# Output passes summed on TensorE by an identity product, gate and residual in the last pass, and five input buffers in place of a staging pool

## The chip, the core and the metric

The kernel runs on one core of one Trainium2 chip. A core has five engines that run side by side: TensorE (PE: matrix products; PEld: the loading of their weights), VectorE (DVE), ScalarE (ACT), GpSimd (POOL) and SyncE (SP), which here issues every DMA, all through one queue. The metric is the device time of one execution in microseconds.

## The reference, cut to what matters

One layer of a hybrid diffusion backbone: a shared input projection, eight head groups ("slots") that each hold a gated DeltaNet head of 128 channels and two RWKV-7 heads of 64, in both directions over time, and a shared output projection. The 256 context tokens pass first and leave the recurrent state from which the 512 latent tokens go on.

```python
h  = rmsnorm(x, norm_g) * (1 + scale) + shift        # 512 x 2048
hc = rmsnorm(ctx, norm_g) * (1 + scale_c) + shift_c  # 256 x 2048
u, uc = h @ w_in, hc @ w_in
ya_c, ya = gdn_mixer(uc[:, :GDN_COLS], u[:, :GDN_COLS], ...)
yb_c, yb = rwkv_mixer(uc[:, GDN_COLS:], u[:, GDN_COLS:], ...)
x = x + gate * (concat([ya, yb]) @ w_out)            # 512 x 2048
return rmsnorm(x, final_norm_g)
```

Only the latent tokens are returned, so the context tokens have no output projection.

## The kernel before, in words

**Layout.** Channels lie on the partitions, tokens in the free dimension. A big product is split for precision: weights and data are each a high and a low part (`wh`, `wl`; `hhi`, `hlo`; `yh`, `yl`), and three products `hi*hi + hi*lo + lo*hi` are added up in PSUM, for every block of 128 input channels, as 128 x 512 pieces.

**Who sets the order.** The code does not write instructions directly. Every call is recorded as an operation with its data dependences, and a planner (`Rec.schedule`) then sorts the operations of each engine by a simulated start time from its own tables of costs; `emit` writes them out in that order. So all instructions have the one line L705, and the order on an engine is fixed by the planner. Each engine runs its list strictly in order. Three tables matter here: `LAT` holds what the planner adds when one engine waits for another, `OWN` what it adds when an operation waits for an earlier one on its own engine (before: V, A and G only, so a DMA that waits for another DMA is planned as if it could go at once), and the `warm` operation: where the planner sees TensorE's recent activity fall below a level it puts in small filler products of zeros (`wm<-zero`).

**Phases.** The front makes the modulation, the norms and the small projections (to some 150 us). The context phase (to some 1000 us) computes the projections `Gk, Gv, Rk, Rv` of every slot for both streams and runs the eight context mixers. The latent phase takes the other projections and the eight latent mixers, slots 0 to 7.

**A mixer** (`Mix`) has these steps: `prep_g`, `prep_r`, `prep_d 0/1`, `blocks 0/1` make small matrices in the tile `Z`; `send` writes their diagonal blocks to DRAM (`DA`); `solve` reads them back (`solNL<-DA`), inverts them on VectorE with 60 dependent elementwise operations (`solT`, `solNL`) and writes the result to DRAM (`DD<-solNL`); `levels` loads it (`lt<-DD`, `Z<-DD`) and finishes the inverses; `chain` walks the eight chunks of time, a serial ping-pong of TensorE, ScalarE, VectorE and GpSimd; `outp` normalizes and stores the result `y`. Two "lanes" of buffers let two neighbouring slots overlap.

**The inputs of a latent mixer.** A projection job (`proj`) collects its sum in PSUM, finishes it in a staging tile (`ul`, a pool of two buffers) and writes it to DRAM (`ud`). Some jobs are done in two parts, and part 1 loads part 0 back into the staging tile. `u_load` loads the six inputs of a slot, in the order Rk, Gk, Rr, Gv, Gq, Rv, into the pool `u` of three buffers (traced as `Rk`).

**The output projection** is cut into four passes over the input channels, each a sweep over the 16 blocks of output channels; pass p takes two slots' channels. Passes 0, 1, 2 are queued after slots 3, 5, 6 as work to fill holes, pass 3 after slot 7's chain in program order, and `out_last` does the last slot. Passes 0 to 2 take for each block an evacuation on ScalarE that also scales by the gate (`xt<-accl`), a load of the running sum (`xr`, in pass 0 of the input x), an addition on GpSimd (`xt<-xt,xr`) and a store (`rtd<-xt`). The same passes split their weights on GpSimd (`wl<-wr,wh`). Pass 3 loads the sum into `rt` and adds its part on VectorE.

Of the kernel before, what the change touches and what calls it, by code (L numbers as in the profile page):

```python
# [7 lines left out]
F32 = mybir.dt.float32  # L8
# [7 lines left out]
P = 128  # L16
# [132 lines left out]
OWN = {"V": 120, "A": 148, "G": 107}  # L149
# [1091 lines left out]
class Kernel:  # L1241
# [51 lines left out]
    def setup(self):  # L1293
# [3 lines left out]
        self.hl = self.pool("hl", side="right")  # L1297
        self.hc = self.pool("hc", side="right")
# [60 lines left out]
    def front(self):  # L1359
# [59 lines left out]
        for kt in range(KT):  # L1419
# [12 lines left out]
            ar = fp.tile([P, 256], F32, tag="ar", bufs=2, name=self.nm("ar"))  # L1432
# [40 lines left out]
        self.ul = self.pool("ul")  # L1473
# [104 lines left out]
    def bcast_rows(self, dst, col, nj, ones, pool, psum):  # L1578
        for g in range(0, nj, 4):
            m = min(4, nj - g)  # L1580
            ps = psum(g // 4)
            for j in range(m):
                dg = pool.tile([P, P], F32, tag="dg", bufs=2, name=self.nm("dg"))
                self.V.tensor_scalar_mul(dg, self.cs("ident"), col[:, g + j:g + j + 1])
                self.mm(ps[:, 128 * j:128 * j + 128], ones, dg)
            self.act(dst[:, 128 * g:128 * (g + m)], ps[:, 0:128 * m], AF.Copy)
# [14 lines left out]
    def proj(self, kind, i, ctx, lat, part=None):  # L1601
# [19 lines left out]
        if lat:  # L1621
            t = self.ul.tile([P, SEQ], F32, tag="ul", bufs=2, name=self.nm(kind))
# [25 lines left out]
    def u_load(self, kind, i):  # L1648
        tag = "uz" if kind[1] == "z" else "u"
        t = self.u[(kind, i, 1)] = self.mp.tile([P, SEQ], F32, tag=tag, bufs=(3, 1)[tag == "uz"], name=self.nm(kind))  # L1650
        self.S.dma_start(t, self.u_d[JOBS.index(kind), i])
# [87 lines left out]
    def main(self):  # L1739
# [27 lines left out]
        for i in range(NSLOT):  # L1767
# [5 lines left out]
            if i == n0:  # L1773
                self.hl.release()
# [46 lines left out]
    def out_pass(self, p):  # L1821
# [5 lines left out]
        for i in range(KT):  # L1827
# [4 lines left out]
            else:  # L1832
                o = 2 * (i % 2)
                if o == 0:
                    hi, lo = self.split(self.I["wout"][24 + 8 * p + i // 2].rearrange("p (k m) -> p k m", m=P), eng)
            for k in range(n):
                for m, (w, hx) in enumerate(((hi, yh), (hi, yl), (lo, yh))):
                    self.mm(ps, w[:, o + k], hx[:, k], k == 0 and m == 0, k == n - 1 and m == 2)
            g = self.dvo["gt"][:, i:i + 1]
            if p == 3:  # L1840
                r = self.rt[:, i]
                self.S.dma_start(r, self.rt_d[:, i])
                self.stt(r, ps, g, r, ALU.mult, ALU.add)
                continue
            x, r = (self.xp.tile([P, SEQ], F32, tag=t, bufs=2, name=self.nm(t)) for t in ("xr", "xt"))
            self.S.dma_start(x, self.rt_d[:, i] if p else self.I["xt"][:, i, 0:SEQ])
            self.act(r, ps, AF.Copy, scale=g)
            self.tt(r, r, x, ALU.add, self.G)
# [60 lines left out]
    def close(self):  # L1909
# [4 lines left out]
        self.ul.release()  # L1914
# [27 lines left out]
```

## Time and profile before

| | us |
|---|---|
| time, median of 3 runs (lowest to highest) | 2160.66 (2158.78 to 2163.45) |
| time of the profiled execution | 2166.2 |
| its span, first to last instruction | 2164.4 |
| PE busy | 1966.3 (91%) |
| DVE busy | 1475.2 (68%) |
| ACT busy | 815.9 (38%) |
| POOL busy | 640.2 (30%) |
| DMA packets' share of the 16 engines | 41.8% |

The span is the stretch between the first and the last instruction of the profiled execution; its time is the span and 1.8 us around it. "Busy" is the share of the span in which an engine had an instruction of the program under way. PE's 91% holds the filler products too, so it must be read by stage.

### The profile page before, as it was taken

What the parts mean: (1) busy time and instruction counts of PE and PEld (TensorE: products, weight loads), DVE (VectorE), ACT (ScalarE), POOL (GpSimd) and SP (SyncE); (2) the same over time, 40 slices, a digit from 0 to 9 for tenths busy, and PEclk for the clock granted to TensorE, in tenths of its full rate; (3) what the DMA queues carried; (4) which work ended last, traced back from release to release, by engine and by line L of the source; (5) the groups of instructions that cost most, each with busy time, mean ns of one, the idle gap of its engine ahead of it and who ended that gap; (6) DMA issues with size and microseconds to landing.
All of it is one profiled execution on the core that took longest, in us unless ns stands there. A gap on an engine that the chain in (4) does not pass through costs nothing.

```text
span 2164.4 us, 44432 instructions
## 1 busy us (share of the span) xinstructions
PE 1966.3 (91%) x16999; PEld 1542.0 (71%) x17000; DVE 1475.2 (68%) x3397; ACT 815.9 (38%) x2127; POOL 640.2 (30%) x799
## 2 busy tenths in 40 slices
PE   7999999999999999999999999978887897889877
PEld 5678887777877778776777777756665666667666
DVE  6436578675867769574765865786868577767747
ACT  4443333333242433324434434436424452435235
POOL 0003404213140421101212202235823564246226
PEclk8999999999999999999999999999979899899998
DMA  8964433333333333344541542544631544044702
GB/s 305 358 221 109 114 92 95 94 89 88 95 98 90 103 101 88 84 114 124 143 133 47 157 128 67 177 140 143 202 87 44 150 154 136 24 123 123 229 12 97
DMA packets 230517, 269.33 MB, mean 124 GB/s; under 512 B 117280, under 2 KB 130080, under 8 KB 226208
## 3 DMA queue, kind: packets, MB, share of 16 engines
q1 hardware_dynamic: 230304, 266.49, 41.8%
q8 instruction: 133, 2.18, 0.4%
q14 instruction: 80, 0.66, 0.1%
HBM read 210.50 MB, written 55.89 MB: 123 GB/s over the span
## 4 chain that ended last, share of the span: by engine, by line
PE 51%; DVE 22%; DMA 12%; issue 5%; SPq 5%; ACT 3%; POOL 3%; DVEq 0%; ACTq 0%; POOLq 0%
PE accl L705 23%; PE wm L705 8%; PE pss L705 7%; PE br L705 7%; PE accc L705 6%; DVE solNL L705 6%; SPq L705 5%; DVE solT L705 4%; DMA DD<-solNL 3%; DVE Gk L705 3%; DVE wl L705 2%; DMA DA<-Z 1%; DVE t L705 1%; DMA solNL<-DA 1%; DMA yl<-yd 1%
## 5 line engine op out<-in xcount | busy, mean ns | idle before, releaser
L705 ACT ACTIVATE wh<-wr 128x512 fp32r<-128x512 f32 x312 | 196.1, 629 | 375.5 <-PE accc L705 144.3
L705 PE MATMUL accl<-hhi,wl 128*128 128x512 f32 x768 | 317.1, 413 | 10.9 <-DVE wl L705 10.9
L705 PE MATMUL accl<-hhi,wh 128*128 128x512 f32 x768 | 314.1, 409 | 1.8 <-issue 1.8
L705 PE MATMUL accl<-hlo,wh 128*128 128x512 f32 x768 | 312.7, 407 | 0.0
L705 DVE TENSOR_TENSOR wl<-wr,wh 128x512 fp32r<-128x512 f32 x264 | 187.6, 713 | 106.9 <-ACT wh L705 102.5
L705 PE MATMUL accl<-yh,wh 128*128 128x512 f32 x480 | 199.3, 418 | 22.0 <-ACT yh L705 13.8
L705 PE MATMUL accl<-yl,wh 128*128 128x512 f32 x480 | 198.7, 414 | 0.1
L705 PE MATMUL accl<-yh,wl 128*128 128x512 f32 x480 | 197.1, 412 | 1.5 <-DVE wl L705 0.9
L705 PEld LDWEIGHTS accl<-hhi,wl 128*128 128x128 f32 x768 | 146.9, 191 | 50.9 <-DVE wl L705 13.3
L705 DVE TENSOR_TENSOR solNL<-solNL,solT 48x30 f32<-48x30 f32 (+29 forms) x480 | 175.2, 365 | 10.3
L705 DVE TENSOR_TENSOR solT<-solNL 48x30 f32<-48x30 f32 (+29 forms) x480 | 170.6, 355 | 9.0
L705 POOL TENSOR_TENSOR SRd<-Sbd,Dd 64x128 f32<-64x128 f32 x160 | 71.1, 444 | 354.2 <-DVE Sbd L705 348.1
L705 PE MATMUL wm<-zero 128*128 128x128 bf16 x1846 | 146.2, 232 | 30.3 <-DVE SG L705 15.0
L705 PEld LDWEIGHTS accl<-hhi,wh 128*128 128x128 f32 x768 | 146.9, 191 | 20.6 <-issue 4.3
L705 PEld LDWEIGHTS accl<-hlo,wh 128*128 128x128 f32 x768 | 147.0, 191 | 20.2 <-issue 3.2
L705 PEld LDWEIGHTS <-zero 128*128 128x128 bf16 x1864 | 124.4, 105 | 51.7 <-issue 46.6
L705 PE MATMUL accc<-clo,wh 128*128 128x256 f32 x512 | 149.9, 293 | 0.0
L705 PE MATMUL accc<-chi,wh 128*128 128x256 f32 x512 | 147.6, 288 | 0.0
L705 PE MATMUL accc<-chi,wl 128*128 128x256 f32 x512 | 145.9, 285 | 0.0
L705 PEld LDWEIGHTS accl<-yh,wh 128*128 128x128 f32 x480 | 90.9, 191 | 43.2 <-ACT yh L705 15.0
L705 PEld LDWEIGHTS accc<-clo,wh 128*128 128x128 f32 x512 | 97.3, 190 | 24.1 <-issue 0.9
L705 PEld LDWEIGHTS accc<-chi,wh 128*128 128x128 f32 x512 | 97.3, 190 | 21.5 <-issue 0.7
(312 smaller groups left out, 4207.8 us busy)
## 6 DMA issues: line engine op xcount, KB each, us to landing
wr<-win SPq DMA_DIRECT2D x256, 256.0 KB, 3.2
wa<-wada SPq DMA_DIRECT2D x32, 1024.0 KB, 6.0
ud<-Gk SPq DMA_DIRECT2D x72, 256.0 KB, 2.6
gw<-wada SPq DMA_DIRECT2D x64, 256.0 KB, 3.5
wr<-wout SPq DMA_DIRECT2D x64, 256.0 KB, 2.9
Rk<-ud SPq DMA_DIRECT2D x48, 256.0 KB, 3.2
rtd<-xt SPq DMA_DIRECT2D x48, 256.0 KB, 2.2
xr<-rtd SPq DMA_DIRECT2D x32, 256.0 KB, 3.0
```

The lines of the kernel that those rows point to most:

```text
L705: r = getattr(self.engs[o.eng], o.fn)(*args, **kw)
```

## The change

Five edits go together.

1. Passes 1, 2 and 3 first load the running sum into `xr` and add it to the PSUM sum by a product with the identity matrix (`accl<-Rr,cst`; `xr` carries the name `Rr` in the new build), 48 products of 128 x 512 in plain fp32. The evacuation no longer scales, the addition on GpSimd is gone, and pass 0 loads nothing.
2. Gate and residual come once, in pass 3, which now loads the input x into `rt` and does `rt = ps * gate + rt`.
3. The pool `u` has five buffers instead of three. The room comes from the staging pool, which is closed when slot 3 begins; part 1 of a projection job stages in `xr`.
4. The planner's table `OWN` gets 1500 ns for S: a DMA that needs an earlier DMA's data is planned later.
5. `ar` and the `dg` tiles of the front have one buffer instead of two.

```diff
-OWN = {"V": 120, "A": 148, "G": 107}
+OWN = {"V": 120, "A": 148, "G": 107, "S": 1500}
...
+        self.ul = self.pool("ul", side="right")
...
-            ar = fp.tile([P, 256], F32, tag="ar", bufs=2, name=self.nm("ar"))
+            ar = fp.tile([P, 256], F32, tag="ar", bufs=1, name=self.nm("ar"))
...
-                dg = pool.tile([P, P], F32, tag="dg", bufs=2, name=self.nm("dg"))
+                dg = pool.tile([P, P], F32, tag="dg", bufs=1 + (pool.name == "fin"), name=self.nm("dg"))
...
-            t = self.ul.tile([P, SEQ], F32, tag="ul", bufs=2, name=self.nm(kind))
+            pool, tag = (self.xp, "xr") if part == 1 else (self.ul, "ul")
+            t = pool.tile([P, SEQ], F32, tag=tag, bufs=2, name=self.nm(kind))
...
-        t = self.u[(kind, i, 1)] = self.mp.tile([P, SEQ], F32, tag=tag, bufs=(3, 1)[tag == "uz"], name=self.nm(kind))
+        t = self.u[(kind, i, 1)] = self.mp.tile([P, SEQ], F32, tag=tag, bufs=(5, 1)[tag == "uz"], name=self.nm(kind))
...
             if i == n0:
+                self.ul.release()
...
+            if p:
+                x = self.xp.tile([P, SEQ], F32, tag="xr", bufs=2, name=self.nm("xr"))
+                self.S.dma_start(x, self.rt_d[:, i])
+                self.mm(ps, self.cs("ident"), x, True, False)
             for k in range(n):
                 for m, (w, hx) in enumerate(((hi, yh), (hi, yl), (lo, yh))):
-                    self.mm(ps, w[:, o + k], hx[:, k], k == 0 and m == 0, k == n - 1 and m == 2)
+                    self.mm(ps, w[:, o + k], hx[:, k], not p and k == 0 and m == 0, k == n - 1 and m == 2)
             g = self.dvo["gt"][:, i:i + 1]
             if p == 3:
                 r = self.rt[:, i]
-                self.S.dma_start(r, self.rt_d[:, i])
+                self.S.dma_start(r, self.I["xt"][:, i, 0:SEQ])
                 self.stt(r, ps, g, r, ALU.mult, ALU.add)
                 continue
-            x, r = (self.xp.tile([P, SEQ], F32, tag=t, bufs=2, name=self.nm(t)) for t in ("xr", "xt"))
-            self.S.dma_start(x, self.rt_d[:, i] if p else self.I["xt"][:, i, 0:SEQ])
-            self.act(r, ps, AF.Copy, scale=g)
-            self.tt(r, r, x, ALU.add, self.G)
+            r = self.xp.tile([P, SEQ], F32, tag="xt", bufs=2, name=self.nm("xt"))
+            self.act(r, ps, AF.Copy)
             self.S.dma_start(self.rt_d[:, i], r)
```

The planner sorts the whole program anew, so much moves. Counted over the whole lists: the filler products fall from 1846 to 1326, GpSimd loses its 48 additions, TensorE gains the 48 identity products, and the other instructions are the same ones in another order. Three places show how.

**VectorE where the chain of slot 2 ends.** `SV`, `SG`, `VO` are slot 2's chain (its last copy is `SV<-pss`), `ot` its output step, `solT`/`solNL` the solve of slot 3; a solve's rows grow from 96x30 to 96x240 in its middle and shrink to 96x30 again at its end. Before:

```order
L705 TENSOR_TENSOR SG_1_9315<-SGs_0_9317,pss_0_125 128x128
L705 TENSOR_TENSOR Ktok_0_9331<-br_1_130,rk_0_9302 128x512
L705 TENSOR_TENSOR solT_1425<-solNL_1424 96x240
L705 SCALAR_TENSOR_TENSOR VO_0_9332<-wm_0_124,SGN_73,VO_0_9332 128x128 x2
L705 TENSOR_TENSOR solNL_1424<-solNL_1424,solT_1425 96x16x15
L705 COPY SV_0_9345<-pss_0_125 64x128
L705 TENSOR_TENSOR solT_1425<-solNL_1424 96x240
L705 TENSOR_TENSOR solNL_1424<-solNL_1424,solT_1425 96x15x16
L705 TENSOR_TENSOR ot_0_9325<-accc_1_135,osb_0_9313 128x512
```

The same place after:

```order
L705 TENSOR_TENSOR solT_1428<-solNL_1427 96x30
L705 TENSOR_TENSOR Sbd_1429<-SRd_0_9340,pss_0_130 64x2x64 x2
L705 TENSOR_TENSOR SG_0_9338<-SGs_0_9341,wm_0_129 128x128
L705 TENSOR_TENSOR SG_1_9339<-SGs_0_9341,pss_0_130 128x128
L705 TENSOR_TENSOR Ktok_0_9355<-br_1_135,rk_0_9326 128x512
L705 TENSOR_TENSOR solNL_1427<-solNL_1427,solT_1428 96x30
L705 COPY solNL_1427<-solNL_1427 96x1024
L705 SCALAR_TENSOR_TENSOR VO_0_9356<-wm_0_129,SGN_73,VO_0_9356 128x128 x2
L705 COPY SV_0_9369<-pss_0_130 64x128
L705 TENSOR_TENSOR ot_1_9350<-accc_1_140,osb_0_9337 128x512
```

Before, half of slot 3's solve (31 of its 63 instructions) stands behind the end of slot 2's chain; after, the whole solve stands ahead of it. At the end of slot 6's chain the same holds for slot 7's solve: 41 of 63 behind it before, none after. The counts for slots 4, 5 and 6 behind the chain of the slot ahead of them are 17, 43, 17 before and 37, 21, 27 after.

**TensorE in slot 7's chain.** One of the eight chunks, its middle part: `Xs`, `R`, `SV`, `vt` feed the chain's products, `zero` is the filler, `accl` the bank of the output passes. Before:

```order
L705 MATMUL accc_0_134<-vn_0_9322,Z_0_12641 64x128 x2
L705 LDWEIGHTS zero_0_65
L705 MATMUL wm_0_124<-zero_0_65 128x128
L705 MATMUL pss_0_125<-Xs_0_9318,Z_0_12641 64x64 x4
L705 MATMUL wm_0_124<-R_1590_0_9319,Z_0_12641 64x128
```

After:

```order
L705 MATMUL accc_1_140<-vn_0_9346,Z_0_12502 64x128 x2
L705 MATMUL accl_0_144<-Rr_0_12489,cst_60 128x512
L705 MATMUL pss_0_130<-Xs_0_9342,Z_0_12502 64x64 x4
L705 MATMUL wm_0_129<-R_1590_0_9343,Z_0_12502 64x128
```

An identity product of pass 3 stands where a filler stood, ahead of the chain's next products. Before, pass 3 lay wholly ahead of slot 7's chain; after, 53 products of the passes (10 of them the rest of pass 2) and 8 identity products lie between the starts of the first and the last chunk of that chain, and 53 and 8 behind the start of the last (counted on TensorE's list).

**SyncE between slot 4's solve and its levels.** `DD` is the solve's result on its way out, `lt` and `Z` its way back in. Before:

```order
L705 DMA DD_0_119<-solNL_1424 96x2x1024
L705 DMA lt_0_9312<-DD_0_119 32x12x32
```

After:

```order
L705 DMA DD_0_124<-solNL_1427 96x2x1024
L705 DMA DA_1_123<-Z_0_12502 32x12x32
L705 DMA rtd_117<-xt_1_12492 128x512
L705 DMA wr_2_1435<-wout 128x512
L705 DMA Rr_0_12489<-rtd_117 128x512
L705 DMA rtd_117<-xt_0_12491 128x512
L705 DMA wr_0_1433<-wout 128x512
L705 DMA wup_0_9318<-wup 96x512
L705 DMA lr_0_9325<-lorad_114 96x512
L705 DMA lt_0_9336<-DD_0_124 32x12x32
```

Before, nothing stood between the two in any of the eight latent slots; after, there are 2, 3, 6, 1, 8, 5, 5 and 3 DMA issues in slots 0 to 7, some of which wait for ScalarE, TensorE or GpSimd.

## Rows read from the trace of the kernel before

**Rows 1.** Busy time by stretch, all engines: two stretches ahead of the output passes.

```profile
core 0: us, PE busy (x) PEld busy (x) DVE busy (x) ACT busy (x) POOL busy (x), PEclk, DMA share, GB/s
50.00:100.00 50.00, 50.00 (x449) 32.40 (x448) 24.54 (x56) 20.62 (x39) 0.00 (x0) 1.00 0.96 361
...
1300.00:1350.00 50.00, 50.00 (x473) 36.34 (x473) 26.95 (x79) 22.71 (x65) 11.25 (x24) 1.00 0.21 58
```

**Rows 2.** The same view cut at latent chains; columns as above; the sum spans 1469:2055.

```profile
1390.00:1469.00 79.00, 60.95 (x629) 47.12 (x630) 67.38 (x144) 31.95 (x86) 20.40 (x24) 0.94 0.56 164
...
1530.00:1603.00 73.00, 60.23 (x637) 47.47 (x636) 51.79 (x80) 21.81 (x50) 43.74 (x37) 0.88 0.58 169
1603.00:1658.00 55.00, 43.55 (x519) 32.97 (x518) 42.38 (x128) 26.52 (x92) 17.00 (x32) 0.91 0.14 40
...
1835.00:1893.00 58.00, 45.98 (x517) 34.85 (x518) 42.15 (x128) 26.74 (x94) 17.30 (x33) 0.85 0.13 38
...
1989.00:2055.00 66.00, 58.34 (x495) 45.11 (x494) 48.55 (x84) 16.83 (x35) 21.32 (x17) 0.93 0.68 218
2055.00:2103.00 48.00, 37.66 (x475) 28.75 (x474) 17.91 (x68) 14.91 (x43) 8.33 (x20) 0.91 0.01 2
2103.00:2164.40 61.40, 45.09 (x453) 42.95 (x452) 44.66 (x74) 33.58 (x87) 37.92 (x37) 0.87 0.30 95
...
sum 586.00, PE 499.28 PEld 381.41 DVE 421.05 ACT 234.78 POOL 276.67; mean PE 49.93 PEld 38.14 DVE 42.10 ACT 23.48 POOL 27.67
```

**Rows 3.** Instructions of the solve alone (tile solT), by stretch: DVE busy (count).

```profile
1530.00:1603.00 73.00, 19.68 (x31) 0.88 0.58 169
1603.00:1658.00 55.00, 15.73 (x44) 0.91 0.14 40
...
1760.00:1835.00 75.00, 22.99 (x42) 0.93 0.52 153
...
1989.00:2055.00 66.00, 20.55 (x40) 0.93 0.68 218
```

**Rows 4.** DVE and POOL instructions in order of time: start, us, what.

```profile
1539.10 1.49 DVE L705 TENSOR_TENSOR solT<-solNL 96x234 f32<-96x234 f32 x1
...
1538.87 1.46 POOL L705 TENSOR_TENSOR xt<-xt,xr 128x512 f32<-128x512 f32 x1
```

**Rows 5.** Groups by form: busy us, mean ns of one, idle before and its cause.

```profile
L705 PE MATMUL wm<-zero 128*128 128x128 bf16 x1846 | 146.2, 232 | 30.3 <-DVE SG L705 15.0 <-ACT vn L705 6.9 <-ACT vt L705 6.5
...
L705 POOL TENSOR_TENSOR wl<-wr,wh 128x512 fp32r<-128x512 f32 x48 | 67.5, 1409 | 20.3 <-ACT wh L705 14.7 <-PE accl L705 4.8
...
L705 POOL TENSOR_TENSOR xt<-xt,xr 128x512 f32<-128x512 f32 x48 | 63.7, 1327 | 28.6 <-ACT xt L705 17.5 <-issue 8.3 <-DMA xr<-xt 2.0
...
L705 DVE SCALAR_TENSOR_TENSOR rt<-accl,dv,rt 128x512 f32<-128x512 f32 x16 | 11.9, 745 | 3.8 <-PE accl L705 2.6 <-DMA DD<-solNL 0.6 <-DMA rt<-rtd 0.5
```

**Rows 6.** PE in order of time: 31 products lie from the first row to the second.

```profile
1000.52 0.40 PE L705 MATMUL accl<-hhi,wh 128*128 128x512 f32 x1
...
1007.76 0.39 PE L705 MATMUL accl<-hlo,wh 128*128 128x512 f32 x1
...
1621.30 1.12 PE L705 MATMUL br<-t,cst 128*128 128x512 f32 x2
1622.36 0.45 PE L705 MATMUL pss<-Xs,Z 64*64 64x64 f32 x8
```

**Rows 7.** The chain of work that ended last, pieces in order of time: start, us, what.

```profile
1471.36 3.89 DMA Rk<-ud
...
2035.51 4.32 DMA DD<-solNL
```

**Rows 8.** Waits: engine and tile, what for, us in total, times, longest.

```profile
ACT t L705 <- DMA Rk<-ud: 20.3, 8, 4.4
...
PE wm L705 <- DMA lt<-DD: 29.0, 26, 2.6
```

**Rows 9.** DMA issues: count, size, median us from issue to landing.

```profile
xr<-rtd SPq DMA_DIRECT2D x32, 256.0 KB, 3.0
```

More of the change, by code (lines that the diff above doesn't have):

```diff
@@ L1472, in front @@
         self.wp = self.pool("wp")
-        self.ul = self.pool("ul")
         self.upA = self.pool("upA")
@@ L1913, in close @@
         self.mp.release()
-        self.ul.release()
         self.wp.release()
```

## The prediction, on record before the change was run

> **What bounds the kernel now.** I read the busy time by stretch first. Up to about 1390 us TensorE is the bound: between 1300 and 1350 us it is busy in all 50 of 50 us, at full clock [rows 1]. Work added ahead of that point costs its own time. Behind it the picture turns. I cut the rest at the first and the last VectorE instruction of each latent chain; "chain" is the stretch inside, "gap" the one from one chain to the next. TensorE's busy share there holds fillers, so it says little. From 1469 to 2055 us, five chains and five gaps, VectorE is busy in 421 of 586 us [rows 2]. The reader should compare the stretches: 73 us with 51.8 of VectorE, 55 with 42.4, 66 with 48.6. VectorE's idle time is 21, 13 and 17 us in these three, 165 us in all ten, 16.5 in the mean. So each stretch lasts about as long as its VectorE work and some 16 us of hand-overs. Slot 7's chain, with nothing beside it, takes 48 us for 17.9 us of VectorE work: there the ping-pong itself is the length [rows 2].
>
> Next, what opens a gap. The chain of waits runs through a load of the inputs, 3.9 us, and through the write of a solve, 4.3 us [rows 7]. All eight slots begin their preparation (`prep_r` on ScalarE) by waiting for Rk [rows 8]: the three buffers come free only late in the slot ahead. A late preparation is a late solve, and of slots 3 and 7 half the solve and more stands behind the chain of the slot before, in the two gaps of 73 and 66 us.
>
> Last, the output passes disturb VectorE. One solve instruction takes 0.36 us in a stretch without passes (15.73 us for 44), but 0.63, 0.55 and 0.51 us in three with them [rows 3]. The timeline shows why: a `solT` that began at 1539.10 ended at 1540.59, after the GpSimd addition that ran from 1538.87 to 1540.33 [rows 4].
>
> **The change, part by part.** Terms are for the span of 2164.4 us.
>
> *VectorE work that leaves 1469:2055.* In VectorE's order, nearly all of pass 3 now stands behind the start of slot 7's chain: of its 16 updates of 0.745 us [rows 5], 8 weight splits and 2 splits of y, all but two instructions, about 16 us. Seven instructions of slot 3's solve and six of its neighbours stand ahead of slot 2's chain now, about 8 us. By the rule of stretches that is -24 us. Bounds: 0, if the idle time grows instead, and -24.
>
> *Solves that end inside the chain ahead.* In gaps 3 and 7 no solve is left. What such a gap still needs is the write of the solve, its loads and `levels`: slot 7 took 19.5 us from 2035.5 to its chain at 2055. The rule would leave these gaps some 36 us (slot 2's output step and slot 4's preparation) and 27 us. Part of that work does not lie on the path, so I take 28 and 23: -12. Bounds: 0 and -25.
>
> *GpSimd's additions.* 63.7 us leave GpSimd; the splits of weights stay, 67.5 us [rows 5]. The solves lost, against 0.36 us each, 8.6, 8.0 and 6.3 us in three gaps [rows 3], 23 in all; output steps and chains are slowed by the same cause, which these rows do not price. I take -16: a little under half of the 23, and as much again at half weight for the rest. Bounds: 0, if the splits cause all of it, and -28.
>
> *The late start of slot 2's chain.* The order of TensorE has 77 more products ahead of the end of slot 2's `blocks 1`, and 190 more (and 2 identity products) ahead of its chain. A product takes 7.24/31 = 0.234 us [rows 6]. The 77 are 18 us. Against them stand TensorE's waits for the loads of `levels`, 29.0 us over 26 times [rows 8], of which 11 of the 16 solves, about 13 to 20 us, lie ahead; the planner now counts a DMA that waits for a DMA, and puts 20 to 55 products there. I take -13: +5. The other 113 products (26 us) fall into 1390:1469, where TensorE is idle for 18 us [rows 2] and runs fillers besides, and where VectorE has 10 us less to do. I take +4. Together +9; bounds -10 (all waits gone, all products in holes) and +45 (190 products, nothing hidden).
>
> *Pass 3 inside slot 7's chain and behind it.* An identity product in fp32 is two records; the nearest row is a 128x512 product in plain fp32, 1.06 us to the next start [rows 6]. Chain 7 gets 53 products and 8 identity products, 12.4 + 8.5 = 21 us of TensorE. The cover: TensorE was idle for 10 of its 48 us, and half its fillers there go (146.2/1846 = 0.08 us each [rows 5]). Cut into eight pieces it will not fit smoothly: +6. Behind the chain, another 21 us beside slot 7's output step, where TensorE was idle for 16 of 61 us [rows 2] and had 218 fillers (17 us), and some ten more VectorE updates: +6. Together +12; bounds 0 and +30.
>
> *At nothing:* the 32 other identity products (34 us) lie in stretches from which some 350 fillers (28 us) go, with VectorE the bound; without that cover they cost these 34 us. ScalarE does the same number of evacuations. The loads of x and of the sums are as many as before. The single buffers of `ar` and `dg` may cost a hand-over or three near 35 us, where the stream of weights is the bound (DMA share 0.96 at 50:100 [rows 1]): 0, bounds 0 and +3.
>
> Sum: -24 - 12 - 16 + 9 + 12 = -31. The profiled execution took 2166.2 us, so 2135 for it; it lies 5.5 us above the median of the runs, and against the median of 2160.7 the forecast is 2130 us (-1.4%).
>
> [...] The chains of slots 3 and 5 hold the same 128 VectorE instructions (42.4 and 42.2 us), yet take 55 us at a granted clock of 0.91 and 58 us at 0.85 [rows 2]: about 0.5 us for each 0.01. [...]
>
> **The rivals.**
>
> *A, the clock falls (slower or no gain).* Place: chains 3 and 5 and gaps 4 and 6, where order shows some 100 fillers fewer and almost no products. Price: 0.5 us for 0.01 in each of four stretches; a fall by 0.15 in all four costs 30 us and eats the gain. Against it: two of these stretches already run at 0.85 to 0.88 and cost only 3 us. Time 2155 to 2170.
>
> *B, SyncE's queue holds up `levels` (slower).* After the solve's write, `lt` used to be issued next; now 1 to 8 other DMAs stand between. Eight issues of some 0.4 us fit into the 4.3 us that the write takes [rows 7], but stores of the passes wait for ScalarE there, and an identity product in the middle of a chain chunk waits for its 3.0 us load [rows 9], with the chain's products queued behind it. If slots 4 to 7 each lose d us, it decides at d = 31/4, about 8 us; at 12 us each the time is 2130 + 48 = 2178. For it: nothing stands in reserve on that queue. Against it: the planner expects about as long a DMA as the rows show.
>
> *C, the solves only change places (no change).* Gaps 4 and 6 get 37 and 27 solve instructions behind the chain where they had 17. If these gaps grow to what gap 5 is now, 75 us, from 42 and 40, they take back 33 and up to 35 of what gaps 3, 5 and 7 give: 2155 to 2165.
>
> *D, the hand-overs shrink too (more gain).* Earlier inputs may take 3 to 5 us of idle time out of each of ten stretches, and GpSimd's relief may reach its bound: 2070 to 2100.
>
> **How the numbers follow.** A difference under 0.2%, 4.3 us, cannot be told from none. My forecast (2101 to 2154): 0.64. D: 0.14. C: 0.08. A: 0.06. B: 0.08. The time is that of the likeliest, 2130. The range from 2086 to 2163 leaves out about half of D, B, and a part of A. Faster: 0.64 + 0.14 and a quarter of A and C, 0.81; same 0.07; slower 0.12.
>
> **What would show it.** Right: gaps 3 and 7 of 20 to 35 us, slot 2's chain starting within 20 us of 1469, solve instructions of slots 3 and 7 nearer to 0.45 us, chain 7 between 50 and 58 us. The work term is wrong if VectorE's idle time per stretch rises above 18 us; the start term if slot 2's chain begins after 1495; A if the clock in chains 3 and 5 is under 0.8; B if TensorE's waits for `lt` or for the identity product's input grow to several us each. A chain 7 above 65 us would make the forecast wrong by itself.

## The result and the profile after

The changed kernel takes 2066.4 us in the median of four runs (2062.8 to 2071.3) against 2162.1 (2158.8 to 2168.2) before: a ratio of 0.9556, 95% interval 0.9525 to 0.9586. The forecast was faster, by 31 us, with a range down to 2086; it became faster by 96 us. The sign held, the size did not.

| | before | after |
|---|---|---|
| span of the profiled execution | 2164.4 | 2063.4 |
| first instruction of slot 0's `blocks 1` on VectorE | 1057.8 | 1019.8 |
| start of slot 2's chain | 1469 | 1466.5 |
| start of slot 2's to start of slot 7's chain | 586 | 474.2 |
| slot 7's chain | 48 | 54.8 |
| behind it | 61.4 | 67.9 |
| mean granted clock of the span | 0.955 | 0.977 |

The first fence is the busy time by stretch of the changed kernel, cut at its latent chains (columns as in [rows 2]): chain 2, gap 3, chain 3, gap 4, gap 5, chain 5, gap 6, gap 7, chain 7, and the rest; the sum is that of the ten stretches from 1466.5 to 1940.7.

```profile
1466.50:1519.40 52.90, 40.51 (x516) 31.68 (x516) 40.72 (x135) 19.77 (x65) 15.03 (x30) 0.90 0.07 18
1519.40:1541.40 22.00, 17.74 (x375) 14.08 (x376) 19.04 (x34) 7.90 (x25) 7.56 (x11) 1.00 0.54 133
1541.40:1591.60 50.20, 42.08 (x523) 31.69 (x522) 40.35 (x115) 25.28 (x82) 21.12 (x34) 0.97 0.25 65
1591.60:1656.10 64.50, 54.62 (x580) 39.98 (x579) 51.81 (x93) 24.08 (x67) 28.58 (x31) 1.00 0.59 166
...
1712.80:1759.10 46.30, 37.01 (x478) 28.27 (x477) 33.53 (x67) 11.11 (x30) 15.02 (x16) 0.86 0.54 143
1759.10:1812.60 53.50, 43.60 (x525) 31.98 (x524) 40.78 (x122) 27.91 (x96) 20.52 (x37) 0.96 0.16 45
1812.60:1862.40 49.80, 42.66 (x495) 32.30 (x494) 39.07 (x74) 14.80 (x37) 20.60 (x20) 0.93 0.53 148
...
1918.30:1940.70 22.40, 21.60 (x291) 15.37 (x292) 10.90 (x19) 8.43 (x22) 7.33 (x8) 1.00 0.85 246
1940.70:1995.50 54.80, 51.12 (x473) 35.29 (x470) 26.74 (x82) 17.69 (x49) 8.37 (x20) 0.94 0.50 166
1995.50:2063.40 67.90, 54.40 (x397) 45.65 (x396) 49.68 (x86) 35.12 (x90) 38.58 (x37) 0.90 0.36 117
...
sum 474.20, PE 409.86 PEld 303.06 DVE 368.10 ACT 199.28 POOL 180.87; mean PE 40.99 PEld 30.31 DVE 36.81 ACT 19.93 POOL 18.09
```

The reader should set three things beside [rows 2]. Gaps 3 and 7 are 22.0 and 22.4 us, where they were 73 and 66. VectorE's work in the ten stretches fell from 421 to 368 us, by 53. And its idle time fell from 165 to 106 us, by 59: the "some 16 us of hand-overs" of a stretch, which the forecast carried over, are 10.6 now. Gap 3 lasts 22.0 us with 19.0 of work.

Not all of the 53 us is work that is gone. The first fence is VectorE's busy time of the kernel before, ahead of slot 2's chain, from there to slot 7's chain, and behind that (busy us, instructions, granted clock, DMA share, GB/s), the second that of the changed kernel; the third and the fourth are GpSimd's weight splits in the same stretches.

```profile
0.00:1469.00 1469.00, 991.59 (x2306) 0.97 0.44 129
1469.00:2055.00 586.00, 421.05 (x950) 0.92 0.43 127
2055.00:2164.40 109.40, 62.58 (x142) 0.89 0.17 54
```

```profile
0.00:1466.50 1466.50, 1007.11 (x2317) 0.99 0.46 137
1466.50:1940.70 474.20, 368.10 (x914) 0.96 0.39 109
1940.70:2063.40 122.70, 76.42 (x167) 0.92 0.42 139
```

```profile
0.00:1469.00 1469.00, 4.00 (x3) 0.97 0.44 129
1469.00:2055.00 586.00, 63.46 (x45) 0.92 0.43 127
```

```profile
0.00:1466.50 1466.50, 30.22 (x19) 0.99 0.46 137
1466.50:1940.70 474.20, 39.59 (x29) 0.96 0.39 109
```

VectorE has 53 us less in the middle stretch, but 15 more ahead of it and 14 more behind it: 24 less in the whole span (1475.2 to 1451.6). Of the 48 weight splits of passes 0 to 2, 19 now run ahead of slot 2's chain (3 before), beside slot 2's solve, whose 63 instructions take 34.3 us instead of 24.6.

TensorE's own waits show what changed ahead of all this. The first fence is the busy time of TensorE in the context phase of the kernel before (busy us, instructions, granted clock, DMA share, GB/s), two stretches of 10 us inside it and then the whole; the second is TensorE's instructions in order of time around two waits, the third the sum of such waits in the 820 us (us, times, longest).

```profile
600.00:610.00 10.00, 7.52 (x129) 0.80 0.46 98
610.00:620.00 10.00, 10.00 (x80) 0.86 0.42 124
...
200.00:1020.00 820.00, 781.57 (x5833) 0.98 0.37 98
```

```profile
603.03 0.39 PE L705 MATMUL accl<-hhi,wh 128*128 128x512 f32 x1
...
605.82 0.24 PE L705 MATMUL wm<-lt,Z 32*32 32x32 f32 x2 [1.63 <-DMA lt<-DD]
606.91 0.84 PE L705 MATMUL wm<-lt,Z 32*32 32x32 f32 x42 [0.85 <-DMA lt<-DD]
...
608.28 0.63 PE L705 MATMUL accl<-hhi,wh 128*128 128x512 f32 x1
```

```profile
PE wm L705 <- DMA lt<-DD: 9.6, 10, 1.6
```

TensorE waits 1.6 and 0.9 us for a load, and the granted clock of that stretch and the next is 0.80 and 0.86; a product `accl<-hhi,wh` takes 0.39 us ahead of the waits and 0.63 behind them. In 820 us TensorE is idle for 38 us, of which the waits for `lt` are 9.6; the mean clock of 0.98 is worth, by an estimate from these numbers, another 0.02 x 820 = 16 us. The same stretch of the changed kernel has a clock of 1.00, with one hundred microseconds at 0.98, and in all its span TensorE waits for `lt<-DD` three times, 2.6 us (26 times, 29.0 us before, [rows 8]).

### The profile page after: what moved, and what is told of

It is laid out like the page before. It is cut to its first block, busy times and chain, and to the rows that moved or that the text cites. A ratio compares the mean times of both kernels' runs of the same rounds, so it can differ in the third digit from the quotient of the medians.

```text
span 2063.4 us, 43525 instructions
## 1 busy us (share of the span) xinstructions
PE 1932.1 (94%) x16575; PEld 1501.0 (73%) x16576; DVE 1451.6 (70%) x3397; ACT 811.6 (39%) x2127; POOL 575.9 (28%) x751
## 4 chain that ended last, share of the span: by engine, by line
PE 68%; DVE 17%; DMA 6%; issue 3%; ACT 3%; POOL 2%; SPq 1%; DVEq 0%; ACTq 0%; POOLq 0%
PE accl L705 37%; PE accc L705 9%; PE br L705 8%; PE wm L705 7%; PE pss L705 7%; DVE solNL L705 3%; DVE Gk L705 2%; DVE solT L705 2%; DVE t L705 1%; SPq L705 1%; POOL gw L705 1%; DVE Z L705 1%; DMA solNL<-DA 1%; DMA gw<-wada 1%; DVE wl L705 1%
## 5 line engine op out<-in xcount | busy, mean ns | idle before, releaser
L705 PE MATMUL accl<-hlo,wh 128*128 128x512 f32 x768 | 307.9, 401 | 0.0
L705 PE MATMUL accl<-yh,wh 128*128 128x512 f32 x480 | 207.8, 435 | 11.0 <-DVE Rr L705 5.4
L705 DVE TENSOR_TENSOR solNL<-solNL,solT 48x30 f32<-48x30 f32 (+29 forms) x480 | 171.4, 357 | 10.6
L705 DVE TENSOR_TENSOR solT<-solNL 48x30 f32<-48x30 f32 (+29 forms) x480 | 165.8, 346 | 10.0
L705 PE MATMUL wm<-zero 128*128 128x128 bf16 x1326 | 105.8, 232 | 22.8 <-DVE SG L705 7.7
L705 PEld LDWEIGHTS <-zero 128*128 128x128 bf16 x1344 | 91.2, 105 | 40.7 <-issue 36.1
```

What stands on the lines that cost most here:

```text
L705: r = getattr(self.engs[o.eng], o.fn)(*args, **kw)
```

## The experiments

Eighteen kernels ran. In the expectations, VectorE's work and idle time between chains 2 and 7 were added up from single durations, which overlap a little; the rows count overlaps once. So 401 and 72 or 81 us there are 367 and 106 or 119 by the rows below. "The section" is the stretch from the start of slot 2's chain to that of slot 7's. The time is a median of all runs; the four columns on the right come from the one profiled execution, which lies up to 8 us off that median, in b_noadd 17 above it.

| kernel | time, us | ratio, interval | slot 0 `blocks 1` | section | VectorE busy | idle |
|---|---|---|---|---|---|---|
| before | 2162.1 | 1 | 1058 | 586 | 421 | 165 |
| changed | 2066.4 | 0.956 (0.953 to 0.959) | 1020 | 474 | 368 | 106 |
| o_only | 2104.8 | 0.972 (0.968 to 0.976) | 1022 | 513 | 394 | 119 |
| no_own | 2102.9 | 0.972 (0.968 to 0.976) | 1065 | 513 | 377 | 136 |
| i_only | 2107.7 | 0.971 (0.966 to 0.976) | 1058 | 523 | 380 | 143 |
| oldpass | 2101.3 | 0.971 (0.968 to 0.974) | 1023 | 511 | 396 | 115 |
| buf3 | 2070.9 | 0.957 (0.953 to 0.961) | 1023 | 479 | 367 | 112 |
| pool_twin | 2089.7 | 0.966 (0.959 to 0.973) | 1027 | 490 | 384 | 106 |
| pool_dummy | 2141.4 | 0.991 (0.988 to 0.994) | 1029 | 531 | 364 | 167 |
| pool_order | 2137.8 | 0.987 (0.978 to 0.995) | 1023 | 533 | 349 | 184 |
| pool_add | 2129.5 | 0.984 (0.981 to 0.986) | 1025 | 526 | 385 | 141 |
| b_noadd | 2154.4 | 0.995 (0.992 to 0.999) | 1062 | 583 | 386 | 197 |
| noadd | 2084.9 | 0.962 (0.957 to 0.967) | 1022 | 500 | 377 | 123 |
| o_dd | 2142.4 | 0.990 (0.987 to 0.992) | 1021 | 548 | 368 | 180 |
| o_da | 2160.8 | 0.999 (0.996 to 1.001) | 1030 | 562 | 383 | 179 |
| o_ddda | 2158.4 | 0.998 (0.995 to 1.001) | 1019 | 555 | 379 | 177 |
| o_rest | 2150.8 | 0.996 (0.993 to 1.000) | 1055 | 576 | 422 | 154 |
| own3000 | 2064.4 | 0.955 (0.948 to 0.962) | 1022 | 478 | 361 | 117 |
| nofill | 2074.8 | 0.962 (0.955 to 0.968) | 1022 | 493 | 370 | 123 |
| xt4 | 2067.2 | 0.957 (0.951 to 0.964) | 1027 | 483 | 368 | 115 |

### The parts of the change, one at a time

**o_only: the planner's entry alone.**

```diff
-OWN = {"V": 120, "A": 148, "G": 107}
+OWN = {"V": 120, "A": 148, "G": 107, "S": 1500}
```

> The kernel before with the one planner entry S: 1500 and nothing else. Theory P (the gain ahead of slot 0's latent blocks, 38 us in the changed kernel, comes from the planner counting a DMA that waits for a DMA): TensorE's waits for lt between 200 and 1340 us fall from 12.9 to under 3 us, slot 0's blocks 1 begins near 1020 instead of 1058, and the time is 2110 to 2135. Theory R (the room for inputs and the sums in PSUM bring it, the planner only follows): slot 0's blocks 1 stays within 8 us of 1058 and the time is 2150 to 2170.

2104.8 us, 5 below the range of theory P, whose other signs came. Slot 0's `blocks 1` begin 36 us earlier, TensorE has no wait for `lt<-DD` left among those that the trace lists between 200 and 1020 us, and there it is busy for 24 us more, at full clock:

```profile
200.00:1020.00 820.00, 805.33 (x6030) 1.00 0.39 105
```

The rest comes behind it, where gap 3 is 22 us already and idle time falls from 165 to 119. The entry changes no instruction, only the planner's order and with it the number of fillers (1994 for 1846): 56 of the 96 us can be had by order alone.

**no_own: the changed kernel without that entry.**

```diff
-OWN = {"V": 120, "A": 148, "G": 107, "S": 1500}
+OWN = {"V": 120, "A": 148, "G": 107}
```

> The changed kernel without the planner entry S: 1500. Theory P: the 35 to 40 us ahead of slot 0 are lost again, the rest of the gain stays: 2095 to 2115. Theory R: within 8 us of the changed kernel, 2060 to 2075. Rival Q (the parts only work together, since the planner must know of the loads to use the room): over 2125.

2102.9 us, theory P again: the 38 us ahead of slot 0 are gone, the section keeps 73 of its 112 us of gain.

**buf3: three input buffers in the changed kernel.**

```diff
-bufs=(5, 1)[tag == "uz"]
+bufs=(3, 1)[tag == "uz"]
```

> The changed kernel with three buffers for the loaded inputs instead of five, all else as changed. If the two gaps without a solve (slots 3 and 7, 139 us before and 44 after) come from the earlier loads: solve instructions stand in these gaps again and the time is 2090 to 2115. If they come from the planner's entry or from the passes: solves stay ahead, 2060 to 2075.

2070.9 us; the intervals of buf3 and of the changed kernel overlap. The solves of slots 3 and 7 still stand ahead (gaps of 22.3 and 23.2 us). The buffers bring nothing that these runs can tell.

**oldpass: the output passes of before in the changed kernel.**

```diff
-            if p:
-                ...
-                self.mm(ps, self.cs("ident"), x, True, False)
...
-            self.act(r, ps, AF.Copy)
+            self.act(r, ps, AF.Copy, scale=g)
+            self.tt(r, r, x, ALU.add, self.G)
```

> The changed kernel with the output passes of before (a scaled evacuation, a load and an addition on GpSimd in passes 0 to 2, the sum loaded in pass 3), five buffers and the planner's entry kept. Theory of the prediction (the additions slow VectorE, 16 us, bounds 0 and 28; pass 3 in slot 7's chain costs nothing that this undoes): 2078 to 2095, with solve instructions in gaps with passes at 0.5 us and more. Rival (the passes' sums bring nothing on the path): 2060 to 2072. Rival (they bring most of the 60 us of the tail): over 2105.

2101.3 us, between the theory's range and the rival's: the passes' part is worth 35 us here, not 16 and not 60. Gap 7 is 54 us, chain 7 is 43.

**i_only: the passes' part in the kernel before, nothing else** (the diff of the change's edits 1 and 2 alone).

> The kernel before with the passes' part of the change alone (identity products, gate and residual in pass 3): three input buffers, the staging pool where it was, no S entry in the planner. With the buffers and without the entry it was 2102.9. If the buffers bring nothing without the entry either: 2093 to 2113. If earlier inputs are what let the planner place the solves ahead there: over 2120. If the passes' part alone brings only its GpSimd term: 2135 to 2150.

2107.7 us, in the range for buffers that bring nothing. So each of the two parts alone, the entry and the passes, is worth 56 us, and both with three buffers (buf3) 90: 22 less than their sum.

### Which pairs of DMAs the planner must know

**o_dd.** The kernel before, the 1500 ns for readers of DD alone; `late` is new, for the rest the planner is as before.

```diff
+                        if not wr and t.key.startswith("DD"):
+                            late.add(a)
...
+                if eng == "S" and a in late:
+                    lat = 1500
```

> The kernel before, with the 1500 ns of the planner's S entry only for DMAs that read the tile DD (the loads lt and Z of a solve's result), not for any other pair of DMAs. The whole entry took 56 us off. Theory L (TensorE's queue stood behind products whose lt had not landed): most of it comes back, 2103 to 2120, and TensorE's 29.0 us of waits for lt are under 6 us. Theory S (VectorE's queue stood behind the solve whose read-back from DA had not landed, 27.8 us): under 20 us of it, 2142 to 2165.

2142.4 us, just inside the second range, but not for theory S's reason: the front gains as much as with the whole entry (slot 0's `blocks 1` at 1021), but the section has 180 us of idle time, more than before.

**o_da** has `"DA"` in place of `"DD"`.

> The same with the 1500 ns only for DMAs that read the tile DA (the read-back solNL ahead of a solve). Theory L: 2142 to 2165. Theory S: 2103 to 2120, and VectorE's waits for solNL<-DA fall from 27.8 to under 16 us. If both queues count, each run gives about half: 2120 to 2142.

2160.8 us, no change, though the front again gains 28 us: the section and the way to it give them back. In this front TensorE still waits 9.1 us for `lt`, 11 times between 200 and 1020 us, at a granted clock of 1.00 and with 799 us busy: the gain there does not hang on the waits for `lt` alone.

**o_ddda** has both.

> The kernel before with the 1500 ns for DMAs that read DD or DA, and for no others. Alone the one gave 22 us, the other nothing; the whole entry 56. If the planner must know both loads of a solve before its order is right: 2100 to 2116, VectorE's idle time between chains 2 and 7 near 81 us. If the other pairs count (the results y and the inputs, written and read back by DMA): 2130 to 2150, idle time over 110.

2158.4 us, outside both ranges, worse than with DD alone; the idle time of 177 us is what the second theory said, its time is not.

**o_rest** has the condition turned round, all pairs but these two.

> The kernel before with the 1500 ns for all pairs of DMAs but those through DD and DA (so for the results y, the running sums, the inputs and the small rows). The pairs through DD gave 22 us, those through DA and both together nothing that shows. If the rest carries what is missing by itself: 2105 to 2135. If the rest matters only beside the other two: 2145 to 2165, and slot 0's blocks 1 stay near 1058.

2150.8 us, the second theory. No subset of the entry does what the whole does. In the front any knowledge of a solve's loads brings the gain. In the tail the result is not a sum of the parts: the planner makes another order each time, and its idle time is 154, 177, 179, 180 or 119 us. Why the orders of the subsets are that much worse was not taken further.

### GpSimd's additions: running, waiting, or order

**pool_add: the changed kernel with three buffers, and an addition that nothing reads.**

```diff
             self.act(r, ps, AF.Copy)
+            d = self.xp.tile([P, SEQ], F32, tag="xd", bufs=2, name=self.nm("xd"))
+            self.tt(d, r, r, ALU.add, self.G)
```

> The changed kernel with three input buffers (2070.9) plus one GpSimd addition of 128x512 for each block of passes 0 to 2, from the evacuated tile into a tile that nothing reads: the 48 additions are back, but no result, load or store waits for them. Theory G (the additions slow VectorE by their mere running, and that is most of the 35 us that the passes' part brought): 2088 to 2106, solves of slots 3 to 7 over 135 us in sum instead of 134 for the changed kernel's and about 150. Rival W (what brought it is that no evacuation, store or bank waits for GpSimd, and that pass 3 moved): 2066 to 2080.

2129.5 us, 59 over buf3 and above both theories. The evacuation's buffer still waits for the addition here, so the run does not part them.

**noadd: o_only without the addition.**

```diff
             self.act(r, ps, AF.Copy, scale=g)
-            self.tt(r, r, x, ALU.add, self.G)
```

> The kernel before with the planner's S entry (2104.8), without the GpSimd addition in passes 0 to 2: the running sum and the residual are loaded but not added, so passes 0, 1 and the residual are missing from the output. No identity products, nothing else changed. Theory G: the 30 to 40 us of the passes' part come without any identity product, 2062 to 2076. Rival (they come from the new place of pass 3): 2095 to 2108.

2084.9 us, between the two: 20 of the passes' 35 us. The planner made a new order here too, so the run does not tell the additions' running from that order.

**pool_dummy: an addition behind each weight split**, on whose result nothing hangs.

```diff
                 hi, lo = self.split(...)
+                d = self.xp.tile([P, 4, P], F32, tag="xd", bufs=2, name=self.nm("xd"))
+                self.tt(d, lo.bitcast(F32), lo.bitcast(F32), ALU.add, self.G)
```

> The changed kernel with three input buffers (2070.9), plus one GpSimd addition of 128x512 behind each weight split of passes 0 to 2, from the split's own result into a tile that nothing reads. GpSimd has its 48 additions again, but neither an evacuation nor a store nor an evacuation buffer hangs on them (in pool_add the buffer did). Theory G (their mere running beside VectorE is the price): 2086 to 2106, VectorE's work between the starts of chains 2 and 7 at least 15 us above 401. Rival W (the price is that evacuations, stores and buffers wait for them): 2066 to 2080.

2141.4 us, 70 over buf3, and yet VectorE's work is 364 us against buf3's 367. Both theories fail: VectorE did not do more, it waited more (167 us against 112). What had changed besides the additions was the planner's order, so the next two runs part the two.

**pool_twin: buf3's order to the instruction**, the additions put in only when the program is written out.

```diff
             r = getattr(self.engs[o.eng], o.fn)(*args, **kw)
+            if o in self.twin:
+                ...
+                self.engs["G"].tensor_tensor(xd, ..., ALU.add)
```

> The changed kernel with three input buffers (2070.9), its order on every engine kept to the instruction, and the 48 extra GpSimd additions of pool_dummy put in behind the planner's back when the program is written out. Theory G (the additions' mere running is the price): at least 16 us more, 2086 to 2110, solves of slots 3 to 7 clearly longer. Theory N (in pool_dummy it was the planner's new order, not the running): 2066 to 2082.

**pool_order: pool_dummy's order to the instruction**, its additions left out at the same place.

```diff
+            if o in self.twin:
+                continue
             r = getattr(self.engs[o.eng], o.fn)(*args, **kw)
```

> The counterpart: the order that the planner made for pool_dummy (2141.4), but the 48 additions left out when the program is written. Theory N: the time stays, 2120 to 2145. Theory G: it falls to 2070 to 2100. If both have a part, 2100 to 2120.

2089.7 and 2137.8 us. 48 additions more cost 18.8 us in buf3's order (theory G) and 3.6 us, within the scatter, in pool_dummy's; pool_dummy's order alone costs 67 us (theory N). In buf3's order VectorE's work rises from 367 to 384 us in the section, which holds 29 of the additions, and from 1450 to 1484 us in the whole span; that GpSimd's own list grows by 55 us is part of the 18.8 too, and no run takes it apart. The reader can see what such an order does in pool_order's gap 4, from 1608 to 1715 us. The first fence is the busy time of all engines there, the second VectorE's waits (us, times, longest), the third VectorE's and then TensorE's instructions in order of time.

```profile
1608.00:1715.00 107.00, 93.32 (x747) 68.04 (x745) 47.58 (x104) 36.70 (x92) 47.65 (x44) 0.94 0.59 174
```

```profile
DVE Z L707 <- PE br L707: 36.1, 5, 14.7
```

```profile
1635.90 1.29 DVE L707 TENSOR_TENSOR solT<-solNL 96x184 f32<-96x184 f32 x1
1651.57 1.29 DVE L707 TENSOR_TENSOR Z<-br,cstm 128x512 f32<-128x512 f32 x2 [14.37 <-PE br L707]
1652.77 0.34 DVE L707 TENSOR_TENSOR solNL<-solNL,solT 96x184 f32<-96x184 f32 x1
...
1637.05 0.50 PE L707 MATMUL accl<-yl,wh 128*128 128x512 f32 x1 [3.68 <-POOL yl L707]
1638.75 2.08 PE L707 MATMUL accl<-Rr,cst 128*128 128x512 f32 x2 [0.51 <-ACT xt L707]
...
1650.38 1.16 PE L707 MATMUL br<-KR,BK 64*128 64x128 f32 x16
```

The next step of slot 4's solve (`solNL`, 1652.77) needs nothing that is late. In VectorE's list it stands behind a masked copy of slot 5 (`Z<-br`); that copy's products (`br`) stand in TensorE's list behind the blocks of pass 1, which run from 1637.05 to 1650.38; and these had waited 3.7 us, up to 1637.05, for a split of y on GpSimd. So 14.4 us of VectorE's idle time are a queue behind a queue, and when the second could begin was set by a third. VectorE waits for `br` five times in this gap, 36 us. The gap takes 107 us for 47.6 us of work, where buf3's has 64 for 51.3:

```profile
1597.30:1661.00 63.70, 54.66 (x580) 40.04 (x580) 51.29 (x93) 23.94 (x66) 28.44 (x31) 1.00 0.58 168
```

**b_noadd: the kernel before in its own order, the additions left out when the program is written** (edit as in pool_order, on the additions of the passes).

> The kernel before, its order on every engine kept, with the 48 GpSimd additions of passes 0 to 2 left out when the program is written (so passes 0 and 1 and the residual are missing from the output). The prediction's term for them: 16 us, bounds 0 and 28; pool_twin gave 18.8 in the changed kernel's order: 2136 to 2150. If in the order of before the additions also hold evacuations and banks on the path: under 2130. If they are hidden: 2154 to 2165.

2154.4 us, a ratio of 0.995 (0.992 to 0.999), some 10 us (3 to 18), within the range for additions that are hidden, at its edge. The one profiled execution took 2171.9 us, the longest of its runs, so its idle time may be more than usual. VectorE's instructions of the solve alone (tile `solT`) in the section, first of the kernel before, then of b_noadd; the last row is b_noadd's section with all engines, columns as in [rows 2]:

```profile
1469.00:2055.00 586.00, 133.05 (x300) 0.92 0.43 127
```

```profile
1475.00:2058.00 583.00, 112.71 (x300) 0.92 0.43 127
...
1475.00:2058.00 583.00, 495.10 (x5407) 380.37 (x5406) 386.11 (x949) 234.36 (x657) 209.00 (x278) 0.92 0.43 127
```

The same 300 instructions take 20 us less, VectorE's work in the section falls by 35 us, and the section is 3 us shorter: in this order, kept as it was, nearly all of the freed time turns into waiting. The same holds between pool_dummy and pool_order (15 us less work, 17 more of idle time), but not between pool_twin and buf3 (17 less work, section 11 shorter).

### The other rivals, and better versions

**nofill: no filler products behind the first** (the line that arms them, `warm = o`, is taken out).

> The changed kernel without any filler product behind the first one, so that only real work holds TensorE's clock. Rival A of the prediction (fewer fillers cost clock): the granted clock between chains 2 and 7 falls from 0.96 to under 0.85 and, at 0.5 us per 0.01 in each of ten stretches, the time is 2110 to 2160. If the real products are enough: clock within 0.03 of the changed kernel's, 2055 to 2080.

2074.8 us: 8 us more, with a granted clock of 0.84 in the section instead of 0.96. The clock is the first theory's, the time the second's. By the price that I had worked out, 0.12 less in ten stretches should cost 60 us; in the profiled executions the section is 18 us longer and the span 16, in the medians the kernel 8. Chains 2, 3 and 5 of nofill run at 0.73, 0.90 and 0.84 instead of 0.90, 0.97 and 0.96 and last 3.0, 2.8 and 1.4 us longer, 0.1 to 0.4 us for each 0.01. All this is net: the fillers that are gone had 106 us of TensorE's time.

**own3000: 3000 ns in the entry**, and **xt4: three input buffers, four evacuation buffers.**

> The changed kernel with 3000 ns in place of 1500 in the planner's S entry. If the gain needs only an order that counts those waits at all: 2055 to 2080. If the planner's order in the tail is so sensitive that any change of a number moves the time by tens of us: outside of that, up to 2110, with VectorE's idle time between chains 2 and 7 off from 72 us by 20 or more.

> The changed kernel with three input buffers and four buffers for the evacuated tile of the output passes instead of two, so that an evacuation on ScalarE waits less for the store of the tile two before. If evacuations that wait for stores (8.9 us in three long waits in the changed kernel) still hold TensorE and the gaps: 2045 to 2062. If not: 2063 to 2078.

2064.4 and 2067.2 us: both as the changed kernel. The first says that 3000 does what 1500 does, so the entry's exact size does not matter between these two; the second that evacuations waiting for stores hold nothing that these runs can tell. No run beat the changed kernel by more than the runs scatter.

## Why the prediction was right and wrong

**What was right.** Pass 3 in chain 7 and behind it was put at 6 + 6 us; it is 6.8 and 6.5 (48 to 54.8, 61.4 to 67.9). The first is partly luck: in o_only and oldpass, with a few products of the passes in it, chain 7 takes 43.2 us at a granted clock of 1.00, not 48 at 0.91, and against these pass 3 costs 11.6 us. Gaps 3 and 7 without a solve were put at 28 and 23 us and are 22.0 and 22.4. The identity products were put at nothing, and TensorE hardly waits for their inputs: each is two records of 0.6 us, and it waits 2.0 us in sum ahead of all 96; no run takes them out by themselves.

```profile
L705 PE MATMUL accl<-Rr,cst 128*128 128x512 f32 x96 | 50.1, 603 | 2.0 <-ACT xt L705 1.2 <-DMA Rr<-rtd 0.7
```

The VectorE work that moves out of the section was put at 24 us; added up from the durations it is 25, of which pass 3 is 17. Shorter instructions, put at 16, make up the other 28 of the 53 us. This is not all the additions' doing: 16 of the weight splits left the section with pass 0, and about 10 us come back ahead of it in slot 2's longer solve.

**The step that failed** is the sentence "So each stretch lasts about as long as its VectorE work and some 16 us of hand-overs", with idle time as a constant of the kernel. It changes with the order, and in one order work can turn into idle time. The table holds much the same work in many orders: 349 to 422 us of VectorE's work, and 106 to 197 us of idle time, which do not go together. b_noadd tests the rule in the order that it was read from: 35 us of work gone, and the section 3 us shorter. By the forecast the section was to shrink by 52 us (24 + 12 + 16); it shrank by 112: 53 by work, 59 by idle time, of which gaps 3 and 7 gave 24 (38 to 14.5 us) and the other eight 35. Rival D, 3 to 5 us for each stretch, came nearest, at 0.14; it was 5.9, the time lies under D's 2070 to 2100, and D's first reason, earlier inputs, is not what the runs show.

The causes, as the runs show them: the entry and the passes' part each make the planner write an order with less idle time (165 us to 119 by the entry, to 143 by the passes, to 112 by both with three buffers). That it is less because fewer queues stand behind queues is shown for one gap, in pool_order, and argued for the rest. The rows of [rows 8] pointed there, and I read them only as TensorE's 29 us. In the section, VectorE's waits for `br` before and after, two fences of VectorE's waits, were

```profile
DVE Z L705 <- PE br L705: 19.7, 13, 7.9
...
DVE lt L705 <- PE wm L705: 16.9, 5, 4.5
```

```profile
DVE Z L705 <- PE br L705: 6.6, 5, 3.3
...
DVE lt L705 <- PE wm L705: 2.9, 2, 2.0
```

27 us less in these two. The first is the wait of pool_order in small. The rest of the 59 us is spread over the chains' own waits and others: VectorE's waits for `pss` ahead of `SV` fell from 23.0 to 9.4 us, for `wm` ahead of `R` from 12.9 to 2.6.

**A second step was mis-sized: the late start of slot 2's chain, +9**, measured -3. It has two halves that were both wrong and nearly cancel. Up to the end of slot 2's `blocks 1` I took 18 us for 77 more products and 13 for waits saved, +5. The products came, and still `blocks 1` end at 1352.9 instead of 1382.3, -29. I had priced the waits for `lt` alone, by their own length; with them went most of TensorE's other idle time and the 16 us that the clock of 0.98 is worth by the estimate above (38 and 16 us in 820, against 15 and none, at a clock of 1.00, in o_only: 39 us less, where slot 0's `blocks 1` begin 36 earlier). From there to the chain I took +4 for 113 more products, and it is +27 (1382.3 to 1469, then 1352.9 to 1466.5): slot 2's solve now runs beside pass 0 and takes 79 us from its first to its last instruction, 57 before.

**The buffers** were said to let the solves begin earlier ("a late preparation is a late solve"). buf3 and i_only contradict it: gap 3 loses its solve by the entry, gap 7 by the passes, and two buffers more are worth 4.5 and 4.8 us, within the scatter.

**The rivals.** A (clock): it rose, 0.91 to 0.97 and 0.85 to 0.96 in chains 3 and 5, with less idle time on TensorE (11.5 to 8.1 us and 12.0 to 9.9); nofill, 8 us slower at 0.84 in the section instead of 0.96, shows how little the clock is worth here, net of the fillers. With TensorE's idle time between 200 and 1020 us down from 38 to 13 us the clock there rose from 0.98 to 1.00, and that of the whole span from 0.955 to 0.977 with 520 fillers fewer. B (SyncE's queue): TensorE's waits for `lt` fell, as said above, and those of the identity products for their load are 0.7 us. C (the solves change places): gaps 4 and 6 did grow, by 22.5 and 9.8 us, together half of the 33 and 35 that C gave them; but gap 5, which C left as it was, fell by 29, with 21 instructions of its solve behind the chain instead of 43.

**The additions.** The term was 16 us, by the reading that the additions slow VectorE. In the order of before, b_noadd gives 10 us (3 to 18), which does not exclude 16; in buf3's order it is 18.8. But the way to the number was another: in b_noadd VectorE's work in the section falls by 35 us, twice the term, and the path takes little of it. The solve's 300 instructions alone take 112.7 us there instead of 133.1; by what means the additions lengthen them no run shows. And what a freed engine is worth depends on who waits for it: 18.8, 10 and 3.6 us in three orders, for 28 to 36 us of VectorE's work over the whole span in each.

Open is which decision of the planner makes the good orders: the subsets of the entry show that it is neither the pairs through DD or DA, alone or together, nor the others alone, and no run here parts it further.

## What to carry to other kernels

Idle time of the engine that bounds a stretch is not a constant to be carried into a forecast: ask for each wait what stands ahead in the waiting engine's list, and ahead of that in the list of the engine waited for. Where a planner writes the order, a change of work has two prices, that of the work in the old order and that of the new order; keep the one fixed and change the other (pool_twin and pool_order) before a cause is named, since here the order was worth 67 us where the work was worth 4 to 19. And where TensorE bounds a stretch, read the granted clock beside the length of its waits: here 20 us with two waits for a load, 1.6 and 0.9 us, had 0.80 and 0.86, and 820 us of o_da with eleven of them, 9.1 us in sum, had 1.00.

## What the runs showed of the hardware

- 48 additions on GpSimd (pool_twin: 55 us in sum) made VectorE's work over the whole span 34 us longer in the same order, and the kernel 18.8. In two other orders they made that work 28 and 36 us longer (pool_dummy against pool_order, the kernel before against b_noadd), and the kernel 3.6 and 10 us longer.
- Without fillers TensorE's granted clock in the section was 0.84 instead of 0.96, and the kernel only 8 us slower, net of 106 us of fillers that TensorE no longer ran.
- Waits of 1.6 and 0.9 us for a load, among products of 32x32, stood at 20 us in which the granted clock was 0.80 and 0.86.
